# RWKV core: gram matrices and the last product of the inverse by head, on four 64x64 tiles of TensorE

## The chip, the cores and the metric

The kernel runs on 1 core of one Trainium2 chip. The metric is the device time of one execution in microseconds (us), as the median of several runs. Times of stretches, instructions and waits come from one profiled execution of the kernel before.

## The reference, cut to what matters

The model has four layers; layers 0 and 3 are retention, layer 1 is an mLSTM, and layer 2 is RWKV-7 time mixing with 16 heads of 64 features, run forwards and backwards over 256 context tokens and then 256 latent tokens. The change touches the recurrence of that layer alone:

```python
def _rwkv_scan(r, w, k, v, a, b, state0):
    ...
    def step(S, inp):
        rt, wt, kt, vt, at, bt = inp
        sa = jnp.einsum('bhij,bhj->bhi', S, at)
        S = S * wt[:, :, None, :] + sa[..., None] * bt[:, :, None, :] + vt[..., None] * kt[:, :, None, :]
        return S, jnp.einsum('bhij,bhj->bhi', S, rt)
    S, ys = lax.scan(step, state0, xs)
```

## The kernel before

All of this is `rk_core`. The 512 tokens are cut into chunks of 64; a chunk is solved as a whole by products of 64x64 matrices per head. A **unit** is one direction, one chunk and one half of the heads: 8 heads, held as 4 pairs `p` of 2 heads `h`, a pair filling 128 partitions. A **group** `n` (0 to 7) has 4 units: two directions and two chunks, for one half of the heads. The program is recorded group by group in the order of `ORDER`:

- **P, preparation** (`prep`, twice for a group): loads of `kk`, `k`, `r`; 8 small products into `g` (L1284); tanh on ScalarE; on VectorE the add L1292, the scan L1293, the products L1300, L1307, L1301 and L1305, which writes the block-diagonal tile `bb` (in the trace `bdA`); `kb` on GpSimd.
- **G and H, grams** (`grams1`, `grams2`, L1327 and L1343): 4 products per unit of a 128x128 block-diagonal stationary matrix with 192 columns. The result of `grams1` is spread by ScalarE into `AD` (4 copies), `off` (2 copies, `q` in the trace) and `RB`, and by VectorE into `RB` (L1336); that of `grams2` into `AK`.
- **I, solve** (`solve`): VectorE masks `AD` (L1372), transposes, and inverts the 16x16 blocks in 28 short steps (L1378, L1379); it ends with two transposes (L1382, L1383).
- **J, whole inverse** (`whole`): five runs of 32x32 products on TensorE (L1394, L1399, L1405, L1411, L1417) with copies between them, which fill the block-diagonal tile `M`; then 4 products per unit of `M` with `RB` into one bank of PSUM (L1423), copied to `G`.
- **T, step** (`step`, one for a unit, of the group before): two DMAs load `V` in block-diagonal form, products L1438 to L1450, the state update `S` on VectorE (L1453), the sum `Y`; every second group of a token tile ends in `finish`.

A product in float32 runs as two passes of TensorE, so 4 products are the x8 of a row. A scheduler puts the recorded instructions of each engine in one fixed order, using its own estimates of their cost; the engines then run these orders and wait for each other by semaphores. Banks of PSUM: `g` has two buffers of two banks, `ps` two of one bank, `pp` two. While the first groups run, the layer's other projections (L255 to L257) fill TensorE; in groups 6 and 7 the modulation weights of the last layer are loaded (`adaw`, 256 KB each) and multiplied (L307).

Of the kernel before, what the change touches and what calls it, by code (L numbers as in the profile page):

```python
# [29 lines left out]
CS, AKN, GN, WN, RBN, KBN = 8, 8, 4, 4, 5, 2  # L30
# [101 lines left out]
class Net:  # L132
# [469 lines left out]
    def mlstm(self, i, j):  # L602
        nc, a = self.nc, self.a
        w_in, w_out = a["ml_w_in"][j], a["ml_w_out"][j]
        with ExitStack() as es:
# [106 lines left out]

            def V(h):
                st["v", h] = self.ml_v(h, xmd)
# [469 lines left out]
    def rk_core(self, es, e0, K, B, xd, h, xx, p1, p0):  # L1184
        nc = self.nc
        mm = nc.tensor.matmul
        pg = self.pool(es, "g2", 1, space=PSUM)
        pool = {}
        tl = lambda tag, n, *shape: pool.get(tag, p1).tile([128, *shape], F32, tag=tag, bufs=n, name=tag)
# [5 lines left out]
        bank = lambda tag: self.pt(tag).rearrange("p (q t) -> p q t", q=4)  # L1195
        two = lambda: pg.tile([128, 4, 256], F32, tag="g2", bufs=2, name="g2")
        copy = lambda o, x: nc.scalar.activation(o, x, ACT.Copy)
        vcopy = lambda o, x: nc.vector.tensor_copy(o, x)
        cat = lambda t: t.rearrange("p h t -> p (h t)")
# [41 lines left out]
        M = pb[:, 4:8].rearrange("p u q h t -> p (u q) h t")  # L1241
# [9 lines left out]
        rAK = Ring([p1.tile([128, 4, 192], F32, tag="AK", bufs=4, name="AK") for _ in range(4)])  # L1251
        S = {}
        Y, bon = {}, {}
        hrk = p1.tile([128, 8, 32], F32, name="hrk")
        for p in range(8):
            nc.vector.tensor_scalar(out=hrk[:, p], in0=K["hs32"], scalar1=K["rk"][:, p:p + 1], scalar2=None, op0=OP.mult)
# [3 lines left out]
        gcopy = copy if ENG[5] & 2 else vcopy  # L1260
# [4 lines left out]
        def prep(d, s0, hf):  # L1265
# [49 lines left out]
            for h in range(2):  # L1315
# [4 lines left out]
            return [dict(d=d, s=s0 + x, hf=hf, ch=chunk(d, s0 + x), W=W[:, :, x], bb=bb[:, x], kb=kb[:, x], Dc=Dc[64:128, :, :, x], P=P, kr=(kd, tile_) if x else None)  # L1320
                    for x in range(2)]

        def grams1(u, b0, AD):
            d, W = u["d"], u["W"]
            g = two()
            for p in range(4):
                mm(g[:, p, 0:192], cat(u["bb"][:, p]), W[:, p], start=True, stop=True)  # L1327
            off = u["off"] = roff.next()
            for q in range(4):
                r, half = slice(32 * q, 32 * q + 32), q % 2  # L1330
                (vcopy if half else copy)(AD[r, :, b0:b0 + 4].rearrange("p t q -> p q t"), g[r, :, 32 * half:32 * half + 32])
            for h in range(2):
                r = slice(64 * h, 64 * h + 32)
                copy(off[r], g[r, :, 32:64])
            t = u["RB"] = rRB.next()
            nc.vector.tensor_tensor(out=t[:, :, 0:64], in0=g[:, :, 64:128], in1=K["mrb"][:, d].unsqueeze(1).broadcast_to([128, 4, 64]), op=OP.mult)  # L1336
            copy(t[:, :, 64:128], g[:, :, 128:192])

        def grams2(u):
            d, W = u["d"], u["W"]  # L1340
            g = two()
            for p in range(4):
                mm(g[:, p, 0:192], cat(u["kb"][:, p]), W[:, p], start=True, stop=True)  # L1343
            if u["kr"]:

                kr, tile_ = u["kr"]
                key, o = (tile_, u["hf"]), g[:, 2:4, 192:256]
                for p in range(4):
                    j = slice(32 * p, 32 * p + 32)
                    mm(o[j], hrk[:, 4 * u["hf"] + p], kr[:, p], start=True, stop=True, tile_position=(0, 32 * p))  # L1350
                if key not in bon:
                    bon[key] = p1.tile([128, 2, 64], F32, tag="bon", bufs=4, name="bon")
                    copy(bon[key], o)
                else:
                    nc.vector.tensor_tensor(out=bon[key], in0=bon[key], in1=o, op=OP.add)
            t = u["AK"] = rAK.next()
            nc.vector.tensor_tensor(out=t[:, :, 0:128], in0=g[:, :, 0:128], in1=K["mak"][:, d].unsqueeze(1).broadcast_to([128, 4, 128]), op=OP.mult)
            copy(t[:, :, 128:192], g[:, :, 128:192])
# [27 lines left out]
        def whole(units, O1, O2, los):  # L1386

            quarters = [(32 * q, slice(32 * q, 32 * q + 32)) for q in range(4)]
            part = lambda name: tl(name, 1, 16, 32)
            wide = lambda: bank("ps").rearrange("p q t -> p (q t)").rearrange("p (b t) -> p b t", t=32)  # L1390
            ps, Pm = wide(), part("Pm")
            for b in range(16):
                for o, r in quarters:
                    mm(ps[r, b], los[b // 8][r, :, b % 8], O2[r, :, b], start=True, stop=True, tile_position=(o, o))  # L1394
            nc.vector.tensor_tensor(out=Pm, in0=ps, in1=K["m16"][:, 2].unsqueeze(1).broadcast_to([128, 16, 32]), op=OP.add)
            ps, MT = wide(), part("MT")
            for b in range(16):
                for o, r in quarters:
                    mm(ps[r, b], O1[r, :, b], Pm[r, b], start=True, stop=True, tile_position=(o, o))  # L1399
            for q, (o, r) in enumerate(quarters):  # L1400
                (vcopy if q % 2 else copy)(M[r, :, q // 2, 32 * (q % 2):32 * (q % 2) + 32], ps[r])
            ps = wide()
            for b in range(16):
                for o, r in quarters:
                    mm(ps[r, b], Pm[r, b], O1[r, :, b], start=True, stop=True, tile_position=(o, o))  # L1405
            copy(MT, ps)
            ps, Q = wide(), part("Pm")
            low = [(64 * h, slice(64 * h, 64 * h + 32), 64 * h + 32, slice(64 * h + 32, 64 * h + 64)) for h in range(2)]
            for b in range(16):
                for h, (o, r, o2, r2) in enumerate(low):  # L1410
                    mm(ps[r2, b], units[b // 4]["off"][r, b % 4], M[r, b, h, 0:32], start=True, stop=True, tile_position=(o, o2))  # L1411
            for h, (o, r, o2, r2) in enumerate(low):
                (qcopy if h else copy)(Q[r2], ps[r2])
            ps = wide()
            for b in range(16):
                for o, r, o2, r2 in low:
                    mm(ps[r2, b], MT[r2, b], Q[r2, b], start=True, stop=True, tile_position=(o2, o2))  # L1417
            for h, (o, r, o2, r2) in enumerate(low):
                (qcopy if h else copy)(M[r2, :, h, 0:32], ps[r2])
            for m, u in enumerate(units):  # L1420
                ps = bank("ps")
                for p in range(4):
                    mm(ps[:, p], cat(M[:, 4 * m + p]), u["RB"][:, p], start=True, stop=True)  # L1423
                u["G"] = tl("G", GN, 4, 128)
                (gcopy if m % 2 else copy)(u["G"], ps)

        yseen = {}

        def step(u):
            d, s, hf, ch, W, AK, G = u["d"], u["s"], u["hf"], u["ch"], u["W"], u["AK"], u["G"]  # L1430
            s0 = S[d, hf]
            V = rV.next()
            for h in range(2):
                r = slice(64 * h, 64 * h + 64)
                nc.sync.dma_start(V[r, :, h], B["V"][64 * ch:64 * ch + 64].rearrange("s (p h f) -> s p h f", p=8, h=2)[:, u["P"], h])
            ps = bank("pp")
            for p in range(4):
                mm(ps[0:64, p], AK[:, p, 0:64], cat(V[:, p]), start=True, stop=s == 0)  # L1438
                if s:
                    mm(ps[0:64, p], W[:, p, 0:64], cat(s0[:, p]), start=False, stop=True)  # L1440
            R = rR.next()
            for h in range(2):
                (copy if h else vcopy)(R[64 * h:64 * h + 64, :, h], ps[0:64, :, 64 * h:64 * h + 64])
            f_ = bank("pp")
            m = 64 if s == 7 else 128
            for p in range(4):
                mm(f_[0:m, p], AK[:, p, 64:64 + m], cat(V[:, p]), start=True, stop=False)  # L1447
                if s:
                    mm(f_[0:m, p], W[:, p, 64:64 + m], cat(s0[:, p]), start=False, stop=False)
                mm(f_[0:m, p], G[:, p, 0:m], cat(R[:, p]), start=False, stop=True)  # L1450
            if s < 7:
                for h in range(2):
                    nc.vector.tensor_tensor(out=s0[64 * h:64 * h + 64, :, h], in0=f_[64:128, :, 64 * h:64 * h + 64],  # L1453
                                            in1=u["Dc"][:, h].unsqueeze(2).broadcast_to([64, 4, 64]), op=OP.mult)
            key = ch // 2, hf
            if key not in Y:
                Y[key] = pool["Y"].tile([128, 4, 128], F32, tag=f"Y{ch // 2 % 2}{hf}", bufs=1, name="Y")
            y = Y[key][ch % 2 * 64:ch % 2 * 64 + 64]
            yseen[key] = yseen.get(key, ()) + (ch,)
            if yseen[key].count(ch) == 1:  # L1460
                copy(y, f_[0:64])
            else:
                nc.vector.tensor_tensor(out=y, in0=f_[0:64], in1=y, op=OP.add)
            if len(yseen[key]) == 4:
                finish(*key)
# [75 lines left out]
        def H(n, m):  # L1541
            grams2(U[n][m])
# [44 lines left out]
        for n in range(-1, 10):  # L1587
            for x in ORDER.split():
                m = n + int(x[2:] or 0)
# [104 lines left out]
```

## Time and profile before

| what | us |
|---|---|
| median of 3 runs | 2121.55 (2121.2 to 2126.33) |
| the profiled execution | 2119.65 |
| its span, first to last instruction | 2117.9 |
| TensorE busy in the span | 1968.9 (93%) |
| VectorE busy | 1260.9 (60%) |
| ScalarE busy | 919.6 (43%) |
| RWKV core, first gram to the last step's product | about 1175.7 to 1703 |

The stretch of the change is cut below at the ends of L1383, the last transpose of each solve; such a stretch is called **cycle** 0 to 6. In a row of stretches, the busy time of an engine stands beside the length; what is left is that engine's waiting. TensorE's passes overlap, so the time from start to start counts for its throughput, not the duration of one.

### The profile page before, as it was taken

What the parts mean: (1) busy time and instruction counts of PE and PEld (TensorE: products, weight loads), DVE (VectorE), ACT (ScalarE), POOL (GpSimd) and SP (SyncE); (2) the same over time, 40 slices, a digit from 0 to 9 for tenths busy, and PEclk for the clock granted to TensorE, in tenths of its full rate; (3) what the DMA queues carried; (4) which work ended last, traced back from release to release, by engine and by line L of the source; (5) the groups of instructions that cost most, each with busy time, mean ns of one, the idle gap of its engine ahead of it and who ended that gap; (6) DMA issues with size and microseconds to landing.
All of it is one profiled execution on the core that took longest, in us unless ns stands there. A gap on an engine that the chain in (4) does not pass through costs nothing.

```text
span 2117.9 us, 41647 instructions
## 1 busy us (share of the span) xinstructions
PE 1968.9 (93%) x17146; PEld 1676.3 (79%) x17146; DVE 1260.9 (60%) x2296; ACT 919.6 (43%) x1841; POOL 430.5 (20%) x459
## 2 busy tenths in 40 slices
PE   6999999999999989989699998999999898999996
PEld 5888887887777868777567987888898676999995
DVE  4463544446646266676867536777766466665554
ACT  3241423233434555342435436666665342444433
POOL 1000000004300143340700402332322033311001
PEclk9999999999999989999899998999999999999998
DMA  9332434331554564443135521112234630233331
GB/s 302 107 119 92 138 100 130 105 120 60 189 179 130 171 195 134 149 125 112 61 124 166 168 69 48 40 52 60 70 87 135 202 123 1 90 121 110 120 108 42
DMA packets 241550, 246.40 MB, mean 116 GB/s; under 512 B 30992, under 2 KB 200080, under 8 KB 241360
## 3 DMA queue, kind: packets, MB, share of 16 engines
q1 hardware_dynamic: 241360, 243.73, 36.8%
q8 instruction: 135, 2.21, 0.4%
q14 instruction: 55, 0.45, 0.1%
HBM read 216.29 MB, written 27.39 MB: 115 GB/s over the span
## 4 chain that ended last, share of the span: by engine, by line
PE 73%; DVE 12%; DMA 5%; ACT 5%; issue 3%; POOL 2%; SPq 0%; ACTq 0%; DVEq 0%; POOLq 0%
PE pp L255 15%; PE pp L256 15%; PE pp L257 15%; PE po L256 2%; PE ps L82 2%; PE g L1327 2%; PE po L257 2%; PE po L255 2%; PE ps L307 1%; DMA raw<-ada_w 1%; DVE wl L239 1%; PE g L1343 1%; PE pp L1450 1%; PE ps L255 1%; PE pp L1447 1%
## 5 line engine op out<-in xcount | busy, mean ns | idle before, releaser
L239 DVE TENSOR_TENSOR wl<-wraw,wh 128x1024 fp32r<-128x1024 f32 x216 | 269.3, 1248 | 196.1 <-ACT wh L237 186.7
L237 ACT ACTIVATE wh<-wraw 128x1024 fp32r<-128x1024 f32 x216 | 228.5, 1059 | 271.8 <-PE pp L256 129.0
L255 PE MATMUL pp<-hA,wh 128*128 128x512 f32 (+1 forms) x704 | 255.9, 366 | 8.1 <-DVE rp L526 3.0
L256 PE MATMUL pp<-hB,wh 128*128 128x512 f32 (+1 forms) x704 | 255.4, 364 | 0.0
L257 PE MATMUL pp<-hA,wl 128*128 128x512 f32 (+1 forms) x704 | 255.2, 364 | 0.1
L255 PE MATMUL pp<-zh,wh 128*128 128x512 f32 (+1 forms) x620 | 216.7, 352 | 6.5 <-ACT zh L287 6.0
L257 PE MATMUL pp<-zh,wl 128*128 128x512 f32 (+1 forms) x620 | 212.3, 343 | 0.0
L256 PE MATMUL pp<-zl,wh 128*128 128x256 f32 (+1 forms) x512 | 170.8, 334 | 4.4 <-DVE zl L288 2.9
L366 DVE SCALAR_TENSOR_TENSOR x<-pp,mod,x 128x256 f32<-128x256 f32 x192 | 87.0, 480 | 137.2 <-PE pp L257 136.9
L255 PEld LDWEIGHTS pp<-hA,wh 128*128 128x128 f32 x704 | 132.8, 189 | 33.1 <-PE pp L257 3.6
L257 PEld LDWEIGHTS pp<-hA,wl 128*128 128x128 f32 x704 | 133.5, 190 | 24.3 <-issue 1.6
L256 PEld LDWEIGHTS pp<-hB,wh 128*128 128x128 f32 x704 | 133.6, 190 | 22.5 <-issue 1.7
L255 PE MATMUL pp<-wh,hA 128*128 128x256 f32 x512 | 146.4, 287 | 2.0 <-ACT wh L237 1.9
L255 PEld LDWEIGHTS pp<-zh,wh 128*128 128x128 f32 x620 | 119.0, 192 | 34.1 <-ACT zh L287 6.9
L256 PE MATMUL pp<-wl,hA 128*128 128x256 f32 x512 | 145.1, 284 | 0.5 <-DVE wl L239 0.5
L257 PE MATMUL pp<-wh,hB 128*128 128x256 f32 x512 | 145.0, 284 | 0.0
L257 PEld LDWEIGHTS pp<-zh,wl 128*128 128x128 f32 x620 | 119.4, 193 | 19.3 <-issue 6.7
L256 PEld LDWEIGHTS pp<-zl,wh 128*128 128x128 f32 x512 | 99.2, 194 | 18.6 <-issue 5.4
L255 PEld LDWEIGHTS pp<-wh,hA 128*128 128x128 f32 x512 | 97.5, 191 | 5.9 <-issue 2.6
L256 PEld LDWEIGHTS pp<-wl,hA 128*128 128x128 f32 x512 | 97.4, 190 | 1.4 <-DVE wl L239 0.8
L257 PEld LDWEIGHTS pp<-wh,hB 128*128 128x128 f32 x512 | 97.5, 190 | 0.0
L288 DVE TENSOR_TENSOR vl<-pp,vh 128x256 fp32r<-128x256 f32 x64 | 26.9, 421 | 82.4 <-ACT vh L287 82.4
(520 smaller groups left out, 4687.4 us busy)
## 6 DMA issues: line engine op xcount, KB each, us to landing
wraw<-ret_w_in SPq DMA_DIRECT2D x96, 512.0 KB, 3.8
wraw<-ada_w SPq DMA_DIRECT2D x56, 512.0 KB, 4.0
wraw<-ret_w_out SPq DMA_DIRECT2D x32, 512.0 KB, 3.5
wraw<-ml_w_in SPq DMA_DIRECT2D x32, 512.0 KB, 3.8
wraw<-rk_w_rkvg SPq DMA_DIRECT2D x32, 512.0 KB, 3.7
adaw<-ada_w SPq DMA_DIRECT2D x48, 256.0 KB, 4.4
raw<-ada_w SPq DMA_DIRECT2D x16, 512.0 KB, 7.5
wraw<-ml_w_out SPq DMA_DIRECT2D x16, 512.0 KB, 4.5
```

Source lines behind the costliest of these rows:

```text
L82: nc.tensor.matmul(self.sums[32 * j:32 * j + 32, n * HALF:n * HALF + HALF], net.ones[:, 0:32], src, start=c < 4 and n == 0, stop=c >= 4 an ...
L237: nc.scalar.activation(h, t, ACT.Copy)
L239: (nc.gpsimd if self.nsplit % 4 in self.psplit else nc.vector).tensor_tensor(out=l, in0=t, in1=f(h), op=OP.subtract)
L255: mm(ps, lhs[0], rhs[0], start=start, stop=False)
L256: mm(ps, lhs[0], rhs[1], start=False, stop=False)
L257: mm(ps, lhs[1], rhs[0], start=False, stop=stop)
L288: (eng or self.nc.vector).tensor_tensor(out=l, in0=src, in1=f(h), op=OP.subtract)
L307: nc.tensor.matmul(ps[32 * j:32 * j + 32, 0:m].rearrange("p (b q) -> p b q", b=nb), self.csil[:, k, :], raws[k // n][:, k % n, j], start=k ...
L366: self.nc.vector.scalar_tensor_tensor(out=x, in0=ps, scalar=self.gate(i, c, st), in1=x, op0=OP.mult, op1=OP.add)
L1327: mm(g[:, p, 0:192], cat(u["bb"][:, p]), W[:, p], start=True, stop=True)
L1343: mm(g[:, p, 0:192], cat(u["kb"][:, p]), W[:, p], start=True, stop=True)
L1447: mm(f_[0:m, p], AK[:, p, 64:64 + m], cat(V[:, p]), start=True, stop=False)
```

## The change

Every gram and every last product of the inverse is taken apart by head: instead of one 128x128 stationary matrix with zero blocks, two 64x64 blocks on separate tiles of TensorE. For the pairs 2 and 3 the output goes to the other half of the partitions, so that head 0 of pairs 0 and 1 uses the tile (rows 0, columns 0), head 1 the tile (64, 64), and the heads of pairs 2 and 3 the tiles (0, 64) and (64, 0). `AD`, `RB`, `AK` and `M` then hold pairs 2 and 3 with their heads exchanged; the product with `RB` brings `G` back to the old places; `V` is loaded in the exchanged places, with four DMAs of half the size instead of two. The last product of the inverse now takes two units at once: their pairs 0 and 1 into one bank of PSUM, their pairs 2 and 3 into another, with one copy of each, and `G` is one tile for two units.

```diff
+        def gram(g, x, W):
+            for p in (0, 2, 1, 3):
+                for h, r in heads:
+                    o = 64 * (h ^ p // 2)
+                    mm(g[o:o + 64, p, 0:192], x[r, p, h], W[r, p], start=True, stop=True, tile_position=(64 * h, o))
...
-            for p in range(4):
-                mm(g[:, p, 0:192], cat(u["bb"][:, p]), W[:, p], start=True, stop=True)
+            gram(g, u["bb"], W)
...
-            for p in range(4):
-                mm(g[:, p, 0:192], cat(u["kb"][:, p]), W[:, p], start=True, stop=True)
+            gram(g, u["kb"], W)
...
-            for m, u in enumerate(units):
-                ps = bank("ps")
-                for p in range(4):
-                    mm(ps[:, p], cat(M[:, 4 * m + p]), u["RB"][:, p], start=True, stop=True)
-                u["G"] = tl("G", GN, 4, 128)
-                (gcopy if m % 2 else copy)(u["G"], ps)
+            for m in (0, 2):
+                pair = [bank("ps") for _ in range(2)]
+                for x in range(2):
+                    for p in (0, 2, 1, 3):
+                        for h, r in heads:
+                            o = 64 * (h ^ p // 2)
+                            mm(pair[p // 2][o:o + 64, 2 * x + p % 2], M[r, 4 * (m + x) + p, h], units[m + x]["RB"][r, p], start=True, stop=True, tile_position=(64 * h, o))
+                G = tl("G", GN // 2, 2, 4, 128)
+                for y, ps in enumerate(pair):
+                    (gcopy if y else copy)(G[:, :, 2 * y:2 * y + 2], ps.rearrange("p (x q) t -> p x q t", x=2))
...
-                r = slice(64 * h, 64 * h + 64)
-                nc.sync.dma_start(V[r, :, h], B["V"][64 * ch:64 * ch + 64].rearrange("s (p h f) -> s p h f", p=8, h=2)[:, u["P"], h])
+                for q in range(2):
+                    o = 64 * (h ^ q)
+                    nc.sync.dma_start(V[o:o + 64, 2 * q:2 * q + 2, h], src[:, 2 * q:2 * q + 2, h])
```

The scheduler makes another order of it, on all engines. Lines behind the edits stand 1 to 14 higher in the new file (L1293 there is the add L1292, L1401 the add L1395, L1467 the state update L1453).

On VectorE, behind the last transpose of group 1's solve (the start of cycle 1), the order before has the preparation of group 2 at once, with the inverse's add into `Pm` among it:

```order
L1383 STREAM_TRANSPOSE O_11001<-LS 128x1024
L1292 TENSOR_SCALAR em<-em 128x512
L1293 SCALAR_TENSOR_TENSOR em<-creset,em 128x512
L1453 TENSOR_TENSOR S_11355<-pp,Dc 64x4x64 x2
L1300 SCALAR_TENSOR_TENSOR W_10503<-kk,eL_10511 128x8x64
L1307 TENSOR_TENSOR W_10503<-r,eL_10511 128x8x64
L1301 SCALAR_TENSOR_TENSOR kk<-th,kk 128x512
L1395 TENSOR_TENSOR Pm<-ps,cm_9172 128x512
L1305 TENSOR_TENSOR bdA<-kk,em 64x4x2x64 x2
```

The order after has, at the same place:

```order
L1389 STREAM_TRANSPOSE O_11033<-LS 128x1024
L1363 TENSOR_TENSOR AK_11381<-g_11888,cmak 128x4x128
L1467 TENSOR_TENSOR S_11383<-pp,Dc 64x4x64 x2
L1363 TENSOR_TENSOR AK_11382<-g_11905,cmak 128x4x128
L1401 TENSOR_TENSOR Pm<-ps,cm_9172 128x512
L1467 TENSOR_TENSOR S_11387<-pp,Dc 64x4x64 x2
L1198 COPY Pm<-ps 32x512
L1467 TENSOR_TENSOR S_11383<-pp,Dc 64x4x64 x2
L1198 COPY bdB<-ps 32x16x32
L1293 TENSOR_SCALAR em<-em 128x512
L1294 SCALAR_TENSOR_TENSOR em<-creset,em 128x512
```

The whole inverse of group 1, up to its last copy into `M` (`bdB`), and three state updates now stand ahead of group 2's preparation.

On TensorE in cycle 0, the last products of the preparation's second direction (L1284) stand before behind the fourth run of the inverse (L1411), which waits for copies into `M`:

```order
L1405 MATMUL ps<-AD_10515,Pm 32x32 x64
L1411 MATMUL ps<-bdB,q 32x32 x32
L1284 MATMUL g_11713<-ta,ca_9162 128x128
L1284 MATMUL g_11713<-tw,cw_9161 128x128
L1284 MATMUL g_11713<-ta,ca_9162 128x128
L1327 MATMUL g_11752<-W_11336,bdA 128x192 x4
```

In the order after they stand ahead of that run:

```order
L1411 MATMUL ps<-AD_10515,Pm 32x32 x64
L1285 MATMUL g_11759<-ta,ca_9162 128x128
L1285 MATMUL g_11759<-tw,cw_9161 128x128
L1285 MATMUL g_11759<-ta,ca_9162 128x128
L1452 MATMUL pp<-bdB,AK 64x128 x4
L1417 MATMUL ps<-bdB,q 32x32 x32
L1329 MATMUL g_11798<-W_11368,bdA 64x192 x8
```

What moved is the preparation, in front of the wait. On VectorE at the start of cycle 3, the order after again has the inverse (L1401, both copies) ahead of the preparation, with steps and a `finish` between them:

```order
L1389 STREAM_TRANSPOSE O_11033<-LS 128x1024
L1361 TENSOR_TENSOR bon<-bon,g_13282 128x128
L1363 TENSOR_TENSOR AK_11382<-g_13282,cmak 128x4x128
L1401 TENSOR_TENSOR Pm<-ps,cm_9172 128x512
L1467 TENSOR_TENSOR S_11383<-pp,Dc 64x4x64 x2
L1477 TENSOR_TENSOR Y<-pp,Y 64x512
L1467 TENSOR_TENSOR S_11387<-pp,Dc 64x4x64
L1198 COPY Pm<-ps 32x512
L1467 TENSOR_TENSOR S_11387<-pp,Dc 64x4x64
L1477 TENSOR_TENSOR Y<-pp,Y 64x512
L1198 COPY bdB<-ps 32x16x32
L1467 TENSOR_TENSOR S_11383<-pp,Dc 64x4x64 x2
```

Before, the first row behind L1383 there is the preparation's add L1292, and the copy into `bdB` comes after both preparations. In cycles 2, 4, 5 and 6 the order after keeps the preparation ahead of the inverse's copies or among them, and cycle 4 begins with most of its preparation already done in cycle 3.

## Rows read from the trace of the kernel before

**Rows 1.** Stretches cut at L1383's ends: start:end and length, busy time of PE, PEld, DVE, ACT, POOL, clock.

```profile
1175.70:1243.10 67.40, 64.75 (x442) 59.83 (x440) 36.10 (x59) 31.57 (x70) 14.98 (x12) 1.00 0.46 139
1243.10:1322.40 79.30, 70.30 (x915) 61.97 (x914) 33.80 (x70) 39.34 (x102) 17.67 (x21) 0.91 0.18 53
1322.40:1369.30 46.90, 42.02 (x749) 37.91 (x750) 34.70 (x70) 30.11 (x78) 15.15 (x14) 0.89 0.16 45
1369.30:1417.80 48.50, 45.34 (x794) 40.79 (x791) 34.52 (x73) 30.33 (x79) 14.83 (x14) 0.96 0.16 44
1417.80:1474.20 56.40, 53.69 (x852) 49.51 (x852) 44.42 (x88) 37.78 (x98) 17.11 (x15) 0.94 0.22 63
1474.20:1529.60 55.40, 52.72 (x840) 48.45 (x840) 43.50 (x86) 36.47 (x92) 16.84 (x16) 0.94 0.23 68
1529.60:1584.60 55.00, 52.90 (x900) 48.86 (x901) 35.67 (x76) 32.81 (x84) 14.21 (x15) 0.91 0.29 81
1584.60:1634.80 50.20, 47.60 (x863) 42.25 (x861) 35.45 (x75) 27.84 (x71) 15.26 (x16) 0.97 0.36 106
1634.80:1724.20 89.40, 77.74 (x1146) 66.39 (x1146) 42.70 (x83) 29.97 (x61) 4.40 (x6) 0.94 0.52 168
```

**Rows 2.** Chain of waits, pieces: start us, us, engine, tile, line, count of passes.

```profile
1293.16 1.79 PE ps L1423 x16
...
1301.34 1.31 PE g L1327 x8
...
1575.87 1.89 PE g L307 x64
...
1585.45 2.17 PE ps L1394 x128
```

**Rows 3.** TensorE in order of time: start, duration, line, tile shape, at the end of a preparation's products.

```profile
1363.93 0.27 PE L1284 MATMUL g<-tw,cw 64*128 64x128 f32 x1
1363.93 0.27 PE L1284 MATMUL g<-ta,ca 64*128 64x128 f32 x1
1364.04 0.27 PE L1284 MATMUL g<-tw,cw 64*128 64x128 f32 x1
...
1364.83 0.27 PE L1284 MATMUL g<-tw,cw 64*128 64x128 f32 x1
1365.03 0.49 PE L1447 MATMUL pp<-bdB,AK 128*128 128x128 f32 x2
```

**Rows 4.** ScalarE in order of time, cycle 2: the first and the last gram copies.

```profile
1385.03 1.56 ACT L1197 ACTIVATE AD<-g 32x128 f32<-32x128 f32 x4 [1.42 <-PE g L1327]
...
1397.73 0.55 ACT L1197 ACTIVATE q<-g 32x128 f32<-32x128 f32 x2
```

**Rows 5.** VectorE in order of time, cycles 0 and 2; in brackets the wait before and its cause.

```profile
1292.58 1.39 DVE L1305 TENSOR_TENSOR bdA<-kk,em 64x512 f32<-64x512 f32 x2
...
1369.22 0.38 DVE L1292 TENSOR_SCALAR em<-em 128x512 f32<-128x512 f32 x1
...
1387.17 0.42 DVE L1336 TENSOR_TENSOR RB<-g,cmrb 128x256 f32<-128x256 f32 x1 [1.25 <-ACT q L1197]
...
1398.31 0.42 DVE L1336 TENSOR_TENSOR RB<-g,cmrb 128x256 f32<-128x256 f32 x1 [1.73 <-ACT q L1197]
1398.65 0.68 DVE L1372 TENSOR_TENSOR AD<-AD,cm 128x512 f32<-128x512 f32 x1
```

**Rows 6.** TensorE in order of time: the inverse's fourth run in cycle 0.

```profile
1280.59 1.92 PE L1411 MATMUL ps<-bdB,q 32*32 32x32 f32 x64 [4.26 <-ACT bdB L1197]
```

**Rows 7.** TensorE in order of time: the inverse's first and fifth run in cycle 2.

```profile
1370.21 2.23 PE L1394 MATMUL ps<-O,q 32*32 32x32 f32 x128
...
1391.81 1.20 PE L1417 MATMUL ps<-Pm,MT 32*32 32x32 f32 x64
```

**Rows 8.** All DMAs of V: durations on the SP queue, ns, min/median/max.

```profile
L1435 SPq DMA_DIRECT2D bdB<-mV x64: 573/586/679, 1184.2 to 1691.0; - x64
```

**Rows 9.** Chain of waits from 1160 to 1700 us, shares of those 540 us by line.

```profile
by line: PE g L1327 7.5%; PE pp L255 4.7%; issue 4.7%; PE pp L257 4.6%; PE pp L256 4.6%; PE g L1343 4.5%; PE pp L1450 3.7%; PE pp L1447 3.5%; PE pp L1438 3.3%; PE ps L1423 3.1%; DMA adaw<-ada_w 2.9%; ACT bdB L1197 2.8%; ACT AD L1197 2.8%; P
```

More of the change, by code (lines that the diff above doesn't have):

```diff
@@ L1253, in rk_core @@
         Y, bon = {}, {}
+        heads = [(h, slice(64 * h, 64 * h + 64)) for h in range(2)]
         hrk = p1.tile([128, 8, 32], F32, name="hrk")
@@ L1419, in whole @@
                 (qcopy if h else copy)(M[r2, :, h, 0:32], ps[r2])
-            for m, u in enumerate(units):
-                ps = bank("ps")
-                for p in range(4):
-                    mm(ps[:, p], cat(M[:, 4 * m + p]), u["RB"][:, p], start=True, stop=True)
-                u["G"] = tl("G", GN, 4, 128)
-                (gcopy if m % 2 else copy)(u["G"], ps)
+            for m in (0, 2):
[8 more added lines that the diff above has]
+                    (gcopy if y else copy)(G[:, :, 2 * y:2 * y + 2], ps.rearrange("p (x q) t -> p x q t", x=2))
+                for x in range(2):
+                    units[m + x]["G"] = G[:, x]
         yseen = {}
@@ L1432, in step @@
             V = rV.next()
+            src = B["V"][64 * ch:64 * ch + 64].rearrange("s (p h f) -> s p h f", p=8, h=2)[:, u["P"]]
             for h in range(2):
-                r = slice(64 * h, 64 * h + 64)
-                nc.sync.dma_start(V[r, :, h], B["V"][64 * ch:64 * ch + 64].rearrange("s (p h f) -> s p h f", p=8, h=2)[:, u["P"], h])
+                for q in range(2):
+                    o = 64 * (h ^ q)
+                    nc.sync.dma_start(V[o:o + 64, 2 * q:2 * q + 2, h], src[:, 2 * q:2 * q + 2, h])
             ps = bank("pp")
```

## The prediction

> **What bounds the kernel now.** I read first the busy shares of the core cut into cycles. TensorE is busy for 87 to 97% of nearly every cycle, VectorE for 43 to 79% [rows 1]. This looks like a kernel bound by TensorE, and the change takes a good part of TensorE's work away. The second reading is the chain of waits: of its 540 us the two grams have 7.5 and 4.5%, the product with `RB` 3.1%, together 15.1% or 81.5 us [rows 9]. The third is the order of time on VectorE, and it weakens the first two. A cycle is a ring: preparation on VectorE, grams on TensorE, their copies on ScalarE, mask, solve and transposes on VectorE, then the next preparation. In cycle 2 the preparation starts at 1369.22, as the solve before it ends; the mask L1372 starts at 1398.65, 29.4 us later; the next solve ends at 1417.80, after 19.1 us of VectorE alone [rows 1, 5]. Of that cycle VectorE works 34.5 of 48.5 us, and waits 14.0. Over cycles 1 to 6 its waits are 12.2, 14.0, 12.0, 11.9, 19.3 and 14.8, together 84.2 us; in cycle 0 they are 45.5 [rows 1]. Only out of these waits can a cycle become shorter, unless VectorE's work moves elsewhere.
>
> In cycle 2 the gram stage is not even TensorE's: ScalarE's gram copies run from 1385.03 to 1398.28, 13.3 us, and the `RB` products on VectorE wait for ScalarE's `q`, 1.25 and 1.73 us in two of them, not for the product [rows 4, 5]. Faster grams give little there. In cycle 0 it is another matter: TensorE has the other projections to do, and the inverse's fourth run waits 4.26 us for a copy with more work queued behind it [rows 6].
>
> **What the change costs on TensorE.** A gram of four pairs is 8 passes in 1.31 us, 163 ns each; a product with `RB` is 16 passes for two units in 1.79 us, 112 ns each [rows 2]. The new passes are twice as many with a quarter of the matrix in use. Four different tiles at once would be 163/4 = 41 ns per pass, two at once 82. I look for rows of tiles side by side. Two row tiles of 64 (L1284) start in the same instant and the next pair 0.107 us later, 54 ns per pass, so two at once do run [rows 3]; four column tiles of L307 run 64 passes in 1.89 us, 30 ns each, against 112 for the same 128 columns on the whole array [rows 2], so four do too. I take 43 for the gram and 30 for the product with `RB` (bounds 28 and 56). Counted in the program, the gram passes go from 512 to 1024: 83.5 to 44.0 us, -39.4. The passes with `RB` go from 256 to 512: 28.4 to 15.4, -13.0. Each run between other tile shapes costs a switch: after the last pair of L1284 the next shape starts after 0.20 us, where a pair takes 0.107, so some 0.1 us [rows 3]. The new order has 283 such switches on TensorE, the old 214: +7. TensorE's sum is -45.6 us.
>
> **What else it costs.** The DMAs of `V` go from 64 to 128. One takes 573 to 679 ns now [rows 8]; one of half the size takes somewhere between half and all of that, so +0 to +1.2 us per step on SP. The steps run a cycle behind the group they belong to, and this hides it, except in the last four, where it can be 0 to 5 us; I take 0, as TensorE there has 77.7 us of work in 89.4 [rows 1]. Copies of `G` keep their number and size, but both of a pair of units now come after 32 passes instead of 16, 1 us later for the first and nothing for the last. VectorE's work does not change in sum; `RB`, `AK` and `AD` have the same copies.
>
> **What moves.** This I hold for the larger part, since it sets when VectorE is let go. By the two orders, with the durations of the trace, VectorE's work per cycle changes by -3.9, +4.8, -4.8, +20.9, -24.0, +6.2, +2.0, and -1.2 behind cycle 6.
>
> - Start stretch: TensorE is busy 64.75 of 67.40 [rows 1] and loses 64 gram passes of 163 ns for 128 of 43: 10.4 to 5.5. Of these 4.9 I book **-4.5**.
> - Cycle 0: the second direction's products stand ahead of L1411 now, no longer behind its 4.26 us of waiting and 1.92 us of running [rows 6]; the products that write `bb` end at 1293.97 now [rows 5] and can come 6 to 7 earlier. TensorE's saving itself lies in the same waits. Waits **-6.5** (bounds 0 and -12).
> - Cycle 1: the inverse up to the copy into `bdB` now stands ahead of group 2's preparation on VectorE. From the first run of the inverse to the end of the fifth are 22.8 us in cycle 2, with TensorE's other work in it [rows 7]; up to that copy I take 17 as an estimate, and with the tanh and the products behind it 19.5 before the first scan. VectorE has six short instructions for that time, where before it had the preparation. If later waits shrink by as much, it costs nothing; if none do, 19.5. The inverse no longer lies in the middle of the gram stage, which gives about half back: **+10**.
> - Cycle 2: preparation first as before, its grams faster in front of 13.3 us of copies: **-3.5** (bounds 0 and -6).
> - Cycles 3 and 4: in 3 the inverse again comes first, with two steps and the sums `Y` to fill some of the time, so less than in cycle 1; cycle 4 finds its preparation done. Together **+7** (bounds 0 and +15).
> - Cycle 5: VectorE waits 19.3, the most behind cycle 0, with TensorE 52.9 of 55.0 busy [rows 1]. Some 128 gram passes and 64 of `RB` less in their old form save 11 there: **-8** (bounds -3 and -11).
> - Cycle 6: TensorE 47.6 of 50.2, and VectorE's 35.45 become 37.5 [rows 1]: **0** in waits.
> - Behind cycle 6 the weights of the last layer arrive by DMA while L307 multiplies them; VectorE's 1.2 moved out of there gives nothing: **+1** over the cycles.
>
> The sum is -4.5 - 6.5 + 10 - 3.5 + 7 - 8 + 0 + 1 = -4.5. The profiled execution took 2119.65, so 2115.15; it stands 1.9 below the median 2121.55, so **2117** as a median.
>
> **Rivals.** First, *TensorE is the bound after all*, as the busy shares say. Then the whole 45.6 comes through: 2121.55 - 45.6 = 2076. By the chain, the 81.5 us of grams and `RB` products shrink by 47% (39.4 + 13.0 of 111.9), 38 us: 2083. For it speak cycles 3 to 5 with 95 to 96% busy [rows 1]; against it that VectorE's and ScalarE's parts of the ring alone are 13.3 + 19.1 us and the preparation, and that TensorE's passes there are partly filling.
>
> Second, *slower: the serial cycles decide*. In cycles 1 and 3 VectorE idles through the inverse (19.5 and 15), cycle 4 does not give it back, the gain in cycle 0 halves (-3), cycle 5 gives -3, cycle 2 nothing, the start -4.5, the last steps' four DMAs of `V` add up to 5, and small waits at the new, later copies of `G` come to 1. That could reach +31; about half of the uncertain 34.5 of cycles 1 and 3 gives +13.5, **2135**. It decides from the point where those two cycles give back less than some 12 us of the 34.5 that they add.
>
> Third, *the tiles run two at a time*: heads 0 and 1 of a pair lie on different rows of the array and write the same bank of PSUM. Then the gram costs 82 ns per pass, TensorE saves nothing, the switches stay (+7), and the moved order keeps its costs without the -8 and half of the other gains: about **2123**. Against it: the inverse's 32x32 runs use four rows of tiles into one bank and take 17 ns per pass (128 in 2.17) [rows 2], where 32 columns at 0.85 ns each (163/192) would take 27 one row at a time.
>
> The Trainium skill, "TensorEngine Tiling (Array Packing)", section "Restrictions and Gotchas", says that different row tiles cannot access the same PSUM bank at the same time. That is this third case; the row of the 32x32 runs, 17 instead of 27 ns, does not agree with it as a limit on speed, so it has a small chance.
>
> **How the numbers follow.** What a measurement of this kernel can tell from no change is about 0.3%, 6.4 us. The forecast (2108 to 2128) has 0.40, the first rival 0.21, the second 0.29, the third 0.10. Faster than 2115.2: all of the first rival and nearly half of the forecast, 0.21 + 0.19 = 0.40. Slower than 2127.9: the second rival and a little of the third, 0.31. The rest, 0.29, is within. For 8 in 10, the range goes up through the second rival to 2138 and down to 2092, where a third of the first rival is inside.
>
> **What would show it.** Right: gram passes that start every 43 ns and `RB` passes every 30; cycle 0 near 69, cycle 1 near 60, cycle 2 near 41, cycle 3 near 80, cycle 4 near 35; VectorE's longest wait in cycles 1 and 3 standing at the copies `Pm` and `bdB`; a lower busy share of TensorE with much the same length. Its clock is granted at 0.89 to 0.97 in the cycles now, of 2.4 GHz with 1.2 as the lower level [rows 1]; with more idle time it may fall, and that would eat some of the saving. Wrong: gram passes at 82 ns or more; cycles 3 and 5 shorter by their whole TensorE saving; cycle 1 below 50; or VectorE waiting for DMAs of `V`.

## The result: slower by 2.5%

The changed kernel takes 2179.15 us (median of 4, 2177.89 to 2180.55); the kernel before, in the same runs, 2123.94. The ratio is 1.0254, with a 95% interval of 1.0233 to 1.0275. Forecast was 2117, with a range from 2092 to 2138.

The profiled execution of the changed kernel took 2178.94 us, its span 2177.1. Its stretches are cut as in [rows 1], here at the ends of L1389, the last transpose of each solve: start:end and length, busy time of PE, PEld, DVE, ACT, POOL, then the granted clock, DMA share and GB/s.

```profile
1178.30:1245.20 66.90, 64.63 (x516) 56.16 (x516) 36.10 (x59) 32.83 (x72) 14.85 (x12) 1.00 0.45 137
1245.20:1314.30 69.10, 57.89 (x883) 45.82 (x881) 31.08 (x62) 30.95 (x81) 18.43 (x21) 0.80 0.15 46
1314.30:1383.50 69.20, 60.22 (x1008) 49.95 (x1008) 38.58 (x80) 37.82 (x100) 14.90 (x14) 0.90 0.18 49
1383.50:1430.70 47.20, 32.82 (x766) 26.46 (x764) 31.75 (x63) 25.30 (x64) 14.49 (x14) 0.73 0.08 22
1430.70:1528.00 97.30, 76.53 (x1124) 65.59 (x1124) 65.48 (x121) 52.07 (x132) 22.85 (x22) 0.87 0.21 57
1528.00:1566.60 38.60, 27.11 (x714) 20.96 (x714) 22.62 (x49) 17.29 (x45) 9.89 (x9) 0.63 0.08 23
1566.60:1637.30 70.70, 61.58 (x1092) 52.94 (x1092) 43.87 (x85) 40.07 (x100) 18.13 (x16) 0.91 0.31 87
1637.30:1700.20 62.90, 51.77 (x1025) 43.42 (x1026) 35.45 (x80) 31.57 (x82) 14.67 (x16) 0.89 0.34 105
1700.20:1779.50 79.30, 68.82 (x1111) 58.49 (x1112) 39.74 (x76) 28.50 (x58) 4.55 (x6) 0.91 0.54 169
```

Against [rows 1], cycle 0 is 10.2 us shorter. Cycle 1 is 22.3 longer, cycles 3 and 4 together 24.1, cycle 5 15.7, cycle 6 12.7; behind cycle 6 the program gets 10.1 back. VectorE's work in all these stretches is nearly the same (344.7 us, before 340.9); its waits in cycles 1 to 6 (length less busy time) are now 30.6, 15.5, 31.8, 16.0, 26.8 and 27.5, together 148.2 against 84.2. These 64 us are more than the loss: 9.5 us of VectorE's work moved into the same cycles besides, and the start, cycle 0 and the end give 20.8 back. That leaves 52.7 of the 59.3 us between the two profiled executions; the other 6.6 lie outside the core and are not explained.

Cycle 3 shows what a longer wait looks like. VectorE in order of time, from the last transpose of the solve to the next preparation (in brackets the wait before, and what ended it):

```profile
1430.75 0.68 DVE L1363 TENSOR_TENSOR AK<-g,cmak 128x512 f32<-128x512 f32 x1
1433.11 0.69 DVE L1401 TENSOR_TENSOR Pm<-ps,cm 128x512 f32<-128x512 f32 x1 [1.68 <-PE ps L1400]
...
1445.81 0.43 DVE L1467 TENSOR_TENSOR S<-pp,Dc 64x256 f32<-64x256 f32 x1 [9.97 <-PE pp L1464]
...
1452.46 0.70 DVE L1198 COPY bdB<-ps 32x512 f32<-32x512 f32 x1 [4.34 <-ACT bdB L1197]
...
1464.06 0.43 DVE L1293 TENSOR_SCALAR em<-em 128x512 f32<-128x512 f32 x1 [2.30 <-ACT em L1290]
```

Before, the add of the preparation came as the solve ended (for cycle 2 in [rows 5]), in cycle 3 too:

```profile
1417.71 0.38 DVE L1292 TENSOR_SCALAR em<-em 128x512 f32<-128x512 f32 x1
```

Now L1293 comes 33.4 us after the end of the solve (1430.65). TensorE tells why it can't come much sooner. Products of that preparation, in order of time:

```profile
1449.31 0.58 PE L1285 MATMUL g<-tw,cw 64*128 64x128 f32 x1
...
1458.76 0.37 PE L1285 MATMUL g<-tw,cw 64*128 64x128 f32 x1
1458.76 0.37 PE L1285 MATMUL g<-ta,ca 64*128 64x128 f32 x1
1458.97 0.27 PE L1285 MATMUL g<-tw,cw 64*128 64x128 f32 x1
```

The first eight passes start 18.7 us after the solve, behind four of the five runs of the inverse and the products of several steps, which stand first in TensorE's queue; the others start only 28 us after it, behind the fifth run and more steps. ScalarE adds to it: the tanh for that add (L1290) stands in its queue behind the `finish` of the steps (L1507).

```profile
1460.50 0.30 ACT L1507 ACTIVATE rs<-rs,gneps 128x8 f32<-128x8 f32 x1
...
1462.12 0.37 ACT L1290 ACTIVATE em<-g,cw 128x128 f32<-128x128 f32 x1
```

So not only VectorE's place for the preparation moved, its inputs on TensorE and ScalarE did too.

The tiles themselves do what the prediction took them to do. Two grams on TensorE in one piece, and one gram in another place; then the granted clock (the third number from the right) of two stretches inside them:

```profile
1221.89 1.53 PE L1329 MATMUL g<-W,bdA 64*64 64x192 f32 x32
...
1497.82 1.56 PE L1329 MATMUL g<-W,bdA 64*64 64x192 f32 x16 [2.28 <-ACT RB L1197]
```

```profile
1221.80:1223.40 1.60, 1.60 (x34) 1.18 (x33) 0.00 (x0) 1.58 (x5) 0.00 (x0) 1.00 0.23 79
...
1497.80:1498.40 0.60, 0.58 (x8) 0.51 (x12) 0.02 (x1) 0.59 (x2) 0.00 (x0) 0.50 0.92 287
```

32 passes take 1.53 us at 2.4 GHz, 48 ns each with the last one's own duration in it. In the second place the clock is granted at 0.50, which is 1.2 GHz, and 16 passes take as long, 98 ns each. In the first, by the trace's single records, four passes start within 20 ns of each other, and one such four follows the other after 163 ns: four at once, 41 ns per pass.

### The profile page after: what moved, and what is told of

Read it like the earlier page. It is cut to its first block, busy times and chain, and to the rows that moved or that the text cites. A ratio compares the mean times of both kernels' runs of the same rounds, so it can differ in the third digit from the quotient of the medians.

```text
span 2177.1 us, 43298 instructions
## 1 busy us (share of the span) xinstructions
PE 1972.6 (91%) x17914; PEld 1647.6 (76%) x17914; DVE 1267.2 (58%) x2296; ACT 921.1 (42%) x1843; POOL 430.8 (20%) x459
## 4 chain that ended last, share of the span: by engine, by line
PE 70%; DVE 15%; ACT 6%; DMA 4%; issue 4%; POOL 1%; SPq 0%; ACTq 0%; DVEq 0%; POOLq 0%
PE pp L255 16%; PE pp L256 15%; PE pp L257 15%; PE po L256 2%; PE po L257 2%; PE ps L82 2%; PE po L255 2%; PE ps L307 1%; ACT AD L1197 1%; DMA raw<-ada_w 1%; DVE wl L239 1%; PE g L1329 1%; PE ps L255 1%; PE ps L256 1%; PE ps L257 1%
## 5 line engine op out<-in xcount | busy, mean ns | idle before, releaser
L1329 PE MATMUL g<-W,bdA 64*64 64x192 f32 x1024 | 77.5, 395 | 37.2 <-ACT RB L1197 13.7
```

The source lines that it names most:

```text
L1329: mm(g[o:o + 64, p, 0:192], x[r, p, h], W[r, p], start=True, stop=True, tile_position=(64 * h, o))
```

## The experiments

Three theories stood against each other: ORDER (the moved order costs the 55 us), CLOCK (TensorE has less to do, falls to the lower clock level and is slow there) and SPLIT (the small products cost more than they save).

**One: the preparation recorded at high priority, in the changed kernel and in the one before.** The scheduler then puts its first rows at the head of the cycle again.

```diff
-            u = prep(d, n // 2 * 2, n % 2)
+            with self.tc.high_priority():
+                u = prep(d, n // 2 * 2, n % 2)
```

> The changed kernel, with the preparation recorded at high priority: the products, tiles, copies and DMAs are those of the change, but on VectorE every cycle begins with the preparation again (1 to 6 of its instructions stand ahead of the inverse's add in cycles 1 to 6). Theory ORDER (the 55 us come from the moved preparation, which VectorE reaches up to 33 us after the transposes): the waits of VectorE in cycles 1 and 3 shrink to the 12 to 15 us of the kernel before, and the time falls to 2105 to 2130 us, ratio to before 0.99 to 1.005. Theory CLOCK (TensorE with fewer busy passes is granted the half clock for 160 us of the core instead of 65, at most 48 us lost): the order does not help, half clock stays at 130 to 170 us, time 2155 to 2180. If both: 2130 to 2155.

Measured: 2141.08 us, ratio 1.0079 (1.0054 to 1.0105). That is above ORDER's band and inside the one for both. VectorE's waits fall to 19.2 us in cycle 3 but stay at 30.7 in cycle 1, where the copy into `Pm` still stands ahead of most of the preparation, and the lower clock level holds for 120 us of the core.

> The kernel before with the same high priority for the preparation, as a control for the one above: ORDER and CLOCK both expect little, 2115 to 2135, since the preparation stood first in every cycle already. More than 1% off would say that the priority itself moves the time, and the split's own effect is then the difference between the two.

Measured: 2136.07 us, ratio 1.0055 (1.0037 to 1.0074), 1 us above its band. So 38 us of the loss go with the priority, and with one and the same edit the split is only 5 us slower than the dense products. But the edit moves the kernel before by 12 us too: an order is itself worth that much, and a comparison that lets the scheduler choose anew says nothing finer.

**Two: dense products, inverse and steps first.** Nothing is split.

```diff
-            whole(U[n], *O[n])
+            with self.tc.high_priority():
+                whole(U[n], *O[n])
...
-            step(U[n][m])
+            with self.tc.high_priority():
+                step(U[n][m])
```

> The kernel before, with its dense 128x128 products, and the whole inverse and the steps recorded at high priority: on VectorE the inverse's add into Pm stands ahead of the whole preparation in cycles 0, 1, 2, 4, 6. Nothing is split. ORDER: slower by 20 to 60 us, 2140 to 2180. CLOCK: within 10 us of before, since TensorE has all of its old passes, or slower only by what the half clock grows.

Measured: 2193.42 us, ratio 1.0332 (1.0310 to 1.0354), 70 us slower and 13 above ORDER's band. An unfavourable order costs that much without any split. But the lower clock level holds for 140 us from its first gram to its last step, with all of the old passes there (65 us in the kernel before, 160 in the changed one), so this run alone doesn't tell whether the clock is cause or consequence.

**Three: the grams by head on two tiles only.**

```diff
+        def gram(g, x, W):
+            for p in range(4):
+                for h, r in heads:
+                    mm(g[r, p, 0:192], x[r, p, h], W[r, p], start=True, stop=True, tile_position=(64 * h, 64 * h))
...
-            for p in range(4):
-                mm(g[:, p, 0:192], cat(u["bb"][:, p]), W[:, p], start=True, stop=True)
+            gram(g, u["bb"], W)
...
```

> The kernel before with the two grams by head on the two diagonal 64x64 tiles only (no exchange of halves, two DMAs of V, dense last product): twice the passes, two at a time, so about the same time on TensorE (two per 163 ns at full clock). The preparation still begins nearly every cycle. ORDER: 2115 to 2140, near before. [...]

Measured: 2140.21 us, ratio 1.0084 (1.0066 to 1.0102), at the upper end of ORDER's band. The lower clock level holds for 72 us of the core, 65 before. The order moved here as well, so the 16 us are not separated into order and products; the run settles little.

**Four: the order held fixed.** For this the positions of the instructions in the order wanted were written into the kernel as a table, and edges that order without a wait were laid along it. The products with `RB` and the copies of `G` were left out, as the change gives them other buffers; in the old order, TensorE's products behind group 6 were too.

```diff
+def impose(nc, tc):
...
+    for e, s in TABLE.items():
+        at = np.cumsum(np.frombuffer(zlib.decompress(base64.b85decode(s)), np.int16).astype(int))
+        if MODE == "edges":
+            for a, b in zip(at[:-1], at[1:]):
+                tc.add_manual_dep(rec[e][b], rec[e][a].name, info, reason="order")
```

> The changed kernel, with the order of the kernel before forced on VectorE, ScalarE, GpSimd and (to the end of group 6) TensorE by edges that order without a wait; only the last products with RB and the copies of G stand where the scheduler puts them. Products, tiles, buffers and DMAs are those of the change. Theory ORDER (the loss is the moved order; the split in itself saves TensorE's time): faster than before, 2085 to 2118 us, ratio 0.983 to 0.998, VectorE's waits in cycles 1 to 6 at or below the 84 us of before. Theory SPLIT (the loss lies in the products themselves: half clock, switches of tile shape, G for two units at once): 2130 us or more with the old order too. Half clock in the core: ORDER 65 to 110 us, SPLIT 130 us or more.

Measured: 2120.64 us (12 runs), against 2125.11 of the kernel before in these runs, ratio 0.9981 (0.9962 to 0.9999). That is 3 us above ORDER's band and 9 below SPLIT's. VectorE's waits in cycles 1 to 6, 81.2 us, and the lower clock level, 89 us, are as ORDER has them. So SPLIT falls, but the split in itself saves less than ORDER took it to.

> The mirror of it: the kernel before with its dense products, with the order of the changed kernel forced on TensorE, VectorE, ScalarE and GpSimd, except for the products with RB and the copies of G. Nothing is split. ORDER: as slow as the changed kernel or slower by part of TensorE's work that it still has, 2175 to 2215 us, with cycle 3 at 85 us or more. SPLIT: 2115 to 2150.

Measured: 2183.04 us, ratio 1.0284 (1.0260 to 1.0308). The two mirror each other. The dense products in the new order are as slow as the changed kernel, and the split in the old order is 4.5 us faster than before. Cycles 1 to 4 of the dense kernel in the new order, columns as above:

```profile
1312.50:1382.30 69.80, 62.92 (x914) 56.56 (x913) 38.87 (x80) 38.16 (x100) 15.22 (x14) 0.90 0.18 48
1382.30:1430.50 48.20, 36.35 (x672) 32.40 (x670) 31.49 (x64) 25.43 (x64) 14.96 (x14) 0.85 0.09 22
1430.50:1529.40 98.90, 81.81 (x1028) 74.21 (x1028) 65.60 (x122) 52.55 (x132) 22.33 (x22) 0.88 0.20 56
1529.40:1569.90 40.50, 33.82 (x630) 31.32 (x634) 23.64 (x50) 17.52 (x45) 10.46 (x9) 0.71 0.07 21
```

They are 69.8, 48.2, 98.9 and 40.5 us long, the changed kernel's 69.2, 47.2, 97.3 and 38.6. The clock is low with dense products too: 0.85 and 0.71 in cycles 2 and 4, where TensorE works only 36.35 of 48.2 us and 33.82 of 40.5, against 0.96 and 0.94 in [rows 1]. With the split it is lower still (0.73 and 0.63), and the time is nearly the same. So ORDER is shown: the order alone brings the loss, and a lower clock comes with it. How much of the loss the slower passes make up inside that order, no run separates.

A third run left TensorE's order to the scheduler and held the others.

> As the first of these three, but TensorE's order is left to the scheduler; VectorE, ScalarE and GpSimd have the order of before. ORDER, if VectorE's order alone decides: within 10 us of the first. If TensorE's own order (its products for the preparation, which stand late) is what makes VectorE wait: 20 us or more above the first.

Measured: 2143.96 us, ratio 1.0095 (1.0072 to 1.0119), 23 us above the run with TensorE's order held too. So the order in TensorE's queue alone is worth 23 us here. This is not the very order that the changed kernel has there; the late products of the preparation above fit it.

**Five: where the gain stays.** The split in the old order, the start, cycles 0 to 6 and the rest:

```profile
1177.20:1246.60 69.40, 67.18 (x515) 58.40 (x515) 35.72 (x59) 33.49 (x73) 14.00 (x12) 0.95 0.44 134
1246.60:1321.10 74.50, 63.27 (x1006) 52.81 (x1004) 33.65 (x69) 37.47 (x99) 17.64 (x21) 0.91 0.20 58
1321.10:1367.10 46.00, 37.08 (x845) 29.92 (x842) 34.78 (x70) 29.87 (x78) 15.09 (x14) 0.89 0.17 45
1367.10:1414.10 47.00, 39.69 (x886) 32.80 (x884) 34.56 (x73) 30.21 (x79) 14.81 (x14) 0.96 0.17 45
1414.10:1470.80 56.70, 51.70 (x948) 44.16 (x948) 44.65 (x89) 36.95 (x98) 17.41 (x15) 0.88 0.23 62
1470.80:1525.20 54.40, 48.09 (x936) 40.69 (x936) 43.45 (x87) 35.70 (x92) 17.14 (x16) 0.94 0.25 70
1525.20:1580.20 55.00, 47.70 (x999) 41.73 (x1000) 34.92 (x77) 32.85 (x84) 14.18 (x15) 0.94 0.31 84
1580.20:1629.20 49.00, 43.27 (x974) 35.03 (x977) 34.50 (x75) 28.64 (x73) 15.31 (x16) 0.97 0.38 113
1629.20:1724.80 95.60, 82.60 (x1161) 70.31 (x1161) 42.67 (x82) 29.07 (x59) 4.39 (x6) 0.88 0.48 153
```

TensorE is busy 330.8 us in the seven cycles, 33.8 less than in [rows 1]; the cycles together are 382.6 long instead of 391.7. Of 33.8 us, 9.1 became time, 4.8 of them in cycle 0. In this execution the start takes 2.0 of them back and the rest 6.2 (95.6 against 89.4, at a clock of 0.88 instead of 0.94; TensorE's order is not held there). Where the remainder stays, the waits of VectorE from the first to the last solve tell (us in all, times, longest). Of the kernel before:

```profile
DVE RB L1336 <- ACT q L1197: 51.4, 25, 3.2
```

and of the split in the old order:

```profile
DVE RB L1343 <- ACT q L1197: 51.9, 25, 3.3
```

The wait for ScalarE's copies out of the gram is the same within half a microsecond, though a gram's products now take half as long (16 passes of 41 ns against 8 of 163). If ScalarE bounds the stage, fewer copies must show it, and the split must gain more by it than the dense products. Half of the copies into `AD` were left out, in both kernels, with the old order:

```diff
-            for q in range(4):
+            for q in (0, 2):
                 r, half = slice(32 * q, 32 * q + 32), q % 2
                 (vcopy if half else copy)(AD[r, :, b0:b0 + 4].rearrange("p t q -> p q t"), g[r, :, 32 * half:32 * half + 32])
```

> As the split in the old order (2120.6 us), with two of the four copies from a gram into AD left out (the odd quarters of AD keep what was there), so 64 copies of about 0.39 us fewer on ScalarE, 25 us, and nothing else changed. Theory COPIES (ScalarE's copies bound the gram stage, so TensorE's saved time falls into waiting): VectorE's wait for q falls from 52 us by 15 to 22 us and the time to 2098 to 2108. Theory TENSOR (TensorE or VectorE's own work bounds it): 2115 or more.

Measured: 2097.67 us, ratio 0.9892 (0.9862 to 0.9921), at the lower edge of COPIES' band.

> The kernel before, its order forced, with the same 64 copies left out. COPIES, with TensorE next in line behind them: the dense grams then bind, and it gains clearly less than the split, 0 to 12 us (2112 to 2125). COPIES with nothing of TensorE behind: it gains as much as the split, 2102 to 2112. TENSOR: no change, 2118 or more.

Measured: 2115.91 us, ratio 0.9962 (0.9944 to 0.9980). The same wait, of the split and then of the dense kernel:

```profile
DVE RB L1343 <- ACT q L1197: 24.2, 21, 2.0
```

```profile
DVE RB L1336 <- ACT q L1197: 38.2, 26, 3.8
```

The split gains 23 us from its 2120.64, the dense kernel 10 from the 2126.05 of before in these runs (by the ratios 0.9 and 0.4%). The dense trace is of the slowest of ten executions, 2124.2 us, so its row shows less of the gain than the median. ScalarE bounds the gram stage in both. Behind it TensorE comes next in the dense kernel, where ScalarE's first copy waits for the gram, and hardly in the split. The dense kernel, then the split:

```profile
ACT AD L1197 <- PE g L1327: 11.5, 13, 2.5
```

```profile
ACT AD L1197 <- PE g L1329: 1.7, 5, 0.7
```

That fits the smaller gain of the dense kernel; a run that shows it by itself was not made.

**Six: two ways to use that.** First, `RB`'s product recorded ahead of the copies, so that it no longer waits for them:

```diff
+            t = u["RB"] = rRB.next()
+            nc.vector.tensor_tensor(out=t[:, :, 0:64], in0=g[:, :, 64:128], in1=K["mrb"][:, d].unsqueeze(1).broadcast_to([128, 4, 64]), op=OP.mult)
             for q in range(4):
...
-            t = u["RB"] = rRB.next()
-            nc.vector.tensor_tensor(out=t[:, :, 0:64], in0=g[:, :, 64:128], in1=K["mrb"][:, d].unsqueeze(1).broadcast_to([128, 4, 64]), op=OP.mult)
```

> The split in the old order, with RB's product on VectorE recorded ahead of the copies of the same gram, so that it waits for TensorE and no longer for ScalarE's six copies, and ScalarE's copies of that bank wait for it instead; the order on each engine stays. COPIES: VectorE's wait for q goes away in part, ScalarE's last copy (RB) no longer waits, 4 to 15 us faster than 2120.6, so 2105 to 2117. Rival: ScalarE's first copies now wait for VectorE, which is late behind the preparation: 2120 to 2135.

Measured: 2136.23 us, ratio 1.0073 (1.0049 to 1.0096).

> The kernel before, its order forced, with the same exchange. COPIES: gains nearly as much as the split (3 to 12 us), since the wait for copies is the same there, 2112 to 2122. Rival as above: 2125 to 2140.

Measured: 2139.72 us, ratio 1.0079 (1.0055 to 1.0103). The rival was right in both, in the split by 1 us more than its band. ScalarE in the split kernel:

```profile
ACT AD L1197 <- DVE RB L1337: 24.8, 16, 3.3
```

The first copy into `AD` now waits for VectorE, which comes late out of the preparation, and the copies were the bound.

Second, three of the copies moved to VectorE, into the place where it waited:

```diff
-            for q in range(4):
-                r, half = slice(32 * q, 32 * q + 32), q % 2
-                (vcopy if half else copy)(AD[r, :, b0:b0 + 4].rearrange("p t q -> p q t"), g[r, :, 32 * half:32 * half + 32])
+            ad = lambda q: (AD[32 * q:32 * q + 32, :, b0:b0 + 4].rearrange("p t q -> p q t"), g[32 * q:32 * q + 32, :, 32 * (q % 2):32 * (q % 2) + 32])
+            for q in (0, 2):
+                copy(*ad(q))
             for h in range(2):
                 r = slice(64 * h, 64 * h + 32)
                 copy(off[r], g[r, :, 32:64])
+            for q in (1, 3):
+                nc.vector.tensor_copy(*ad(q))
...
-            copy(t[:, :, 64:128], g[:, :, 128:192])
+            nc.vector.tensor_copy(t[:, :, 64:128], g[:, :, 128:192])
```

> The split in the old order, complete again, with three of the seven copies of each first gram (two of the four into AD, and the one into RB) moved from ScalarE to VectorE, right beside RB's product there; ScalarE's other copies of the gram come first. ScalarE loses 96 copies of about 0.39 us, 37 us, and no longer hands a bank to VectorE and takes it back; VectorE gets 96 more of 0.25 to 0.4 us, 24 to 38 us, in the place where it waits 52 us in all. COPIES: the gram stage becomes shorter by 1 to 4 us in each cycle, 2095 to 2115 us, below both kernels. Rival (VectorE becomes the bound of the stage, since the moved copies queue behind its preparation): 2116 to 2135.

Measured: 2113.09 us (10 runs), ratio 0.9945 (0.9926 to 0.9963). It is below the kernel before (2124.00 in these runs) and, by the ratios, below the split in the old order (0.9945 against 0.9981). One unit on VectorE, in cycle 2, and the wait for `q` in all:

```profile
1384.65 0.78 DVE L1343 COPY AD<-g 32x128 f32<-32x128 f32 x2 [0.90 <-ACT q L1197]
1385.45 0.42 DVE L1345 TENSOR_TENSOR RB<-g,cmrb 128x256 f32<-128x256 f32 x1
1385.80 0.41 DVE L1346 COPY RB<-g 128x256 f32<-128x256 f32 x1
```

```profile
DVE AD L1343 <- ACT q L1197: 18.2, 16, 2.5
```

A unit takes 1.6 us there; the waits for `q` are 18.2 us, at most 2.5, where they had been 51.9 and 3.3. The dense products with these copies moved were not run, so how much of the 11 us needs the split is open.

## Why the prediction was wrong

**Right: the reading of what bounds the kernel.** It put VectorE's ring above TensorE's busy share, saw in [rows 4, 5] that the gram stage waits for ScalarE, and gave the grams' speed little there. With the order held, 33.8 us of TensorE became 9.1 of cycles, and fewer copies became time at once. Its first rival, TensorE as the bound (2076 to 2083), fell.

**Right: the prices of the passes.** 41 ns for a gram pass at full clock against the 43 taken, 27 for one with `RB` against 30; four tiles ran at once, and the third rival fell. (Its own sum was off: with the costs of 10, 7 and 1 and half of 4.5, 6.5 and 3.5, it comes to about 2132 and not 2123.) The Trainium skill's rule in "TensorEngine Tiling (Array Packing)", "Restrictions and Gotchas", that different row tiles cannot access one PSUM bank at the same time, does not hold here in that breadth: heads 0 and 1 of a pair are on different row tiles, write one bank in different halves of its partitions, and run at once.

**Right: cycle 0.** Waits 45.5 to 38.0, -7.5, where -6.5 was booked. With the old order held the split alone takes 4.7 off them.

**Wrong: the step of the moved order, in its sizes.** It named the mechanism, for cycles 1 and 3, and gave the first +10 between bounds of 0 and 19.5, because the inverse would no longer lie in the middle of the gram stage and give half back. Next to nothing came back: waits 12.2 to 30.6, +18.4, nearly the upper bound. The longest of them, 13.3 us, stands at the copy into `Pm`, as said. Cycles 3 and 4 got +7 between 0 and 15: waits 23.9 to 47.8, +23.9, beyond the bound. That bound counted the inverse alone; the rows of cycle 3 show steps and a `finish` with waits of their own ahead of the preparation, and the preparation's products late on TensorE besides. The longest wait there, 9.97 us, is for a product of the step, and not at `Pm` or `bdB`, as was said.

**Wrong: cycles 5 and 6.** -8 and 0 in waits were booked, on TensorE's busy share; +7.5 and +12.7 came. The orders of these cycles were said to keep the preparation "ahead of the inverse's copies or among them", and no price was put on "among". In cycle 6 both copies stand ahead of the second preparation, whose add comes 29 us after the solve, where it came after 9 before:

```profile
1654.07 0.70 DVE L1198 COPY Pm<-ps 32x512 f32<-32x512 f32 x1 [5.72 <-ACT Pm L1197]
1660.94 0.70 DVE L1198 COPY bdB<-ps 32x512 f32<-32x512 f32 x1 [6.17 <-ACT bdB L1197]
...
1666.18 0.43 DVE L1293 TENSOR_SCALAR em<-em 128x512 f32<-128x512 f32 x1 [2.56 <-ACT em L1290]
```

The waits at these two copies grew from 0.2 to 7.3 us in cycle 5 and from 1.0 to 11.9 in cycle 6. And the busy share was no measure of what TensorE's speed is worth: with the old order held, cycle 5 kept its 55.0 us. The second rival, which was the mechanism of the moved order, ended at 2135 because it took half of the uncertain 34.5 us; all of it would have given 2152, still too little, as it put -3 on cycle 5 and nothing on cycle 6.

**Wrong in small: start and cycle 2.** -4.5 and -3.5 were booked; the start became 0.5 shorter, and the waits of cycle 2 grew by 1.5. With the old order held the start is 2.0 longer and cycle 2 1.5 shorter.

**Mis-sized: the clock.** That it might fall stood in the last paragraph, without a price. The trace's clock record has the lower level for 160 of 601 us of the core, 65 of 548 before. A gram pass takes twice as long there (98 against 48 ns above), and so TensorE's busy time in cycles 0 to 6 is 367.9 us, 3.3 more than before, in spite of the split. What this cost in time is open: the dense kernel in the new order has the lower level for 126 us and takes as long.

**Also off:** behind cycle 6, where 0 was booked, 10 us came back. The new order had done 3 us of VectorE's work earlier, and TensorE had 9 us less there; which of the two gave it back was not tried.

Why the scheduler chose this order when it was given twice as many products was not tried, nor whether telling it their true cost would have kept the old one.

## What to carry to other kernels

Where a scheduler sets the order, a change of instructions is two changes: take them apart by holding the order fixed, in both directions, before a word is said on the products. When the order moves the head of a serial ring behind other work, book the upper bound of the wait unless a row shows what fills it, count in it all that stands ahead, and look in every engine's queue for the inputs of what moved. Work taken from the busiest engine becomes time only as far as no other engine paces the stage; the wait that stays the same names the one to suspect, and taking work from that engine shows whether it does.

## What the runs showed of the hardware

Halving the DMAs of `V` saved nothing on SP's queue: one took 586 ns in the median before [rows 8], and one of half the size takes 597, so the four of a step hold the queue for 1.2 us more than the two did.

```profile
L1449 SPq DMA_DIRECT2D bdB<-mV x128: 573/597/1466, 1174.5 to 1753.6; - x128
```

A copy of 32x128 out of PSUM into `AD`, which exchanges two axes, takes 0.39 us on VectorE as on ScalarE (0.78 for two, above; 1.56 for four in [rows 4]), nearly as much as one of 128x256 into `RB` on VectorE (0.41). A copy of 32x128 into `q`, which exchanges none, takes 0.28 us on ScalarE (0.55 for two in [rows 4]). So the size alone does not set the time; whether the exchanged axes make the difference was not tried.
